# A log-sum-exp over 128 MB on one core: VectorE weighs and sums 4 MB blocks in one go, with a wider filler matmul, a bf16 pass in the closing check, and batch 6's logarithm at the end

## The chip, the core and the metric

The kernel runs on one core of one Trainium2 chip. The core has five engines that run their own instruction streams and meet at semaphores: TensorE (PE: matmuls, PEld: its weight loads), VectorE (DVE), ScalarE (ACT), GpSimd (POOL) and SyncE (SP, which here only issues DMAs). SBUF is the memory on the core with 128 partitions, PSUM the one that TensorE writes. The metric is the time of one execution on the device, in microseconds (us).

## The reference

```python
B, S, D, H = 8, 2048, 2048, 8          # x: 8 x 2048 x 2048 f32, bias: 8 x 256 f32
x_heads = x.reshape(B, S, H, Dh).transpose(0, 2, 1, 3) + bias[None, :, None, :]
x_tiled = np.repeat(x_heads, 2, axis=2)
mx = x_tiled.max(axis=-1, keepdims=True)
lse = mx.squeeze(-1) + np.log(np.exp(x_tiled - mx).sum(axis=-1))
```

Each row of x has 8 heads of 256 numbers. Each head gets its own bias, and the result is the logarithm of the sum of the exponentials, written twice in a row. 128 MB (134 million bytes) are read and 1 MB is written.

## The kernel before

**Tiles.** A tile is 256 rows of x: 128 partitions with K = 2 rows each, 2 MB. There are T = 64 tiles, 8 to a batch. Two neighbouring tiles make a block of 4 MB; four block buffers (xb) hold eight tiles. Tiles 2 to 41 are loaded as whole blocks (L174), the others one by one or in pieces (L185, L193). SP issues a load only when the buffer's last users are done (last_uses, in load and reload).

**The sum without a maximum.** The kernel takes exp without subtracting the maximum, sums, and takes the logarithm. At the end it looks at the largest and smallest sum (ends_of, L532 and L535; judge) and branches to a slow version (all_again) when they lie too far apart. That branch isn't taken here.

**How a bulk tile (0 to 53, BULK) is split by heads.** The loop over t writes the order out by hand; each engine runs its instructions in that order.

- Heads 0 to 2 go through PE: a matmul with ones and the bias in three bf16 parts puts the bias into PSUM (put_bias, L310), and matmuls with the identity add x (late_heads, L369; f32, so each is two passes). ScalarE exponentiates from PSUM: head 0 with its sum (L380, twice), heads 1 and 2 back into xb (L387).
- Heads 4 to 7 get their bias from POOL (g_add, L419).
- ScalarE exponentiates heads 3 to 7 in place (L425, in later).
- VectorE multiplies head 3 by exp(bias) (L437) and sums heads 1 to 7 (L444). This sum is the last use of the buffer, and SP waits for it.

In step t of the loop the order is: PE's matmuls of t, POOL's add of t, the exponential (L425), multiply and sum of tile **t - 1** (flush of for_pool), the exponentials from PSUM of t (L380, L387), and the bias for t + 1.

**The logarithm of a batch.** Two steps after a batch's last tile, finish turns its sums R with four PE transposes (L504), and ScalarE takes the logarithm of the result (L514). It stands at the end of step t = 8b + 9, so in ScalarE's order it comes ahead of the exponential L425 of tile 8b + 9. ends_of follows on VectorE. After batch 6 (t = 57) one DMA stores the results of batches 0 to 6 (store, L518); batch 7 has its own transpose, logarithm and store (finish_last, L613 to L620).

**The prompt tiles (54 to 63).** They are handled row by row (one of the two rows in each partition, 1 MB, at a time; tile 63 in smaller pieces): heads 0 and 1 by PE and ScalarE (L327, L345, L400), the rest exponentiated in place and weighed and summed head by head on VectorE (weigh, L460), one head or two folded on POOL (L476, L484) and summed on VectorE (L490). In tiles 55 to 63 keep_warm puts three 128-column matmuls a row (L360), whose result nobody reads, into PE's order. From there on the exponentials are not held back by a step.

**The end.** ends_of(7) on VectorE, then judge: a small vector (L548), two matmuls into one row (L547 and L556), a maximum (L557), and every engine loads the verdict and branches.

```python
        fb, at = divmod(t - 2, NBLK)
        if fb >= 0 and at == NBLK - 1:
            finish(fb)
            ends_of(fb)
            if fb == B - 2:
                store()
```

Of the kernel before, what the change touches and what calls it, by code (L numbers as in the profile page):

```python
# [9 lines left out]
F32 = mybir.dt.float32  # L10
BF16 = mybir.dt.bfloat16
I32 = mybir.dt.int32
ACT = mybir.ActivationFunctionType
# [4 lines left out]
K = 2  # L18
KB = 4
BLOCKS = 42  # L20

NBUF = 8
# [2 lines left out]

NEARLY = 5

NWARM = 3

# [16 lines left out]
SPAN_BITS = 60 << 23  # L46
# [16 lines left out]
def kernel(  # L63
# [30 lines left out]
    w_sb = sb.tile([P, D - W1], F32, name="w_sb")  # L94
    ident = sb.tile([P, P], F32, name="ident")
    ones = sb.tile([1, P], F32, name="ones")
    ones3 = sb.tile([3, P], BF16, name="ones3")
    b3 = sb.tile([3, CPE], BF16, name="b3")
    bparts = sb.tile([1, 3, CPE], BF16, name="bparts")
    brest = sb.tile([1, 2, CPE], F32, name="brest")  # L100

    b_far = sb.tile([1, 1], F32, name="b_far")
    one_bits = sb.tile([1, 1], F32, name="one_bits")
    ends = sb.tile([P, 2], F32, name="ends")
    far = sb.tile([P, 1], F32, name="far")
    verdict = sb.tile([1, 1], I32, name="verdict")

    NR = KB * H * NB

    Rx = [sb.tile([P, 1 + NR + 1], F32, name=f"R{b}") for b in range(B)]  # L110
    R = [r[:, 1 : 1 + NR].rearrange("p (k h n) -> p k h n", k=KB, h=H) for r in Rx[:-1]]
    R_last = Rx[-1][:, 1 : 1 + NR].rearrange("p (h n k) -> p h n k", h=H, n=NBLK)
    res = sb.tile([H * NB, B - 1, P, KB, 2], F32, name="res")
    res_last = sb.tile([P, P, 2], F32, name="res_last")
    xbs = [sb.tile([P, KB, D], F32, name=f"xb{i}") for i in range(NBUF // TB)]
    xts = [xb[:, k : k + K] for xb in xbs for k in range(0, KB, K)]
# [18 lines left out]
    def rows_of(t, n=1):  # L135


        b, at = divmod(t, NBLK)
        if b < B - 1:
            blk, i = divmod(at, TB)  # L140
            v = x[b, blk * P * KB : (blk + 1) * P * KB, :]
            return v.rearrange("(p k) d -> p k d", k=KB)[:, i * K : (i + n) * K]
        v = x[b, at * P * K : (at + 1) * P * K, :]
        return v.rearrange("(k p) d -> p k d", k=K)


# [53 lines left out]
    def reload(t):  # L200

        n = t + NBUF
        if n < BLOCKS:
            if n % TB == TB - 1:
                load(n - TB + 1)
        elif n < T:
            load(n)

# [4 lines left out]
    for set_idx, (_name, funcs) in enumerate(get_activation_tables(nc.m.arch).items()):  # L213
        if ACT.Exp in funcs and ACT.Ln in funcs:
# [5 lines left out]
            )  # L220
            break
    nc.scalar.dma_start(out=brow, in_=bias.rearrange("h j -> (h j)").unsqueeze(0))
    for t in range(NBUF):
        load(t)
    nc.vector.memset(ones, 1.0)
    nc.vector.memset(ones3, 1.0)
    make_identity(nc, ident)


    bp = brow[:, 0:CPE]  # L230
# [15 lines left out]
    for i, c in enumerate(range(G0, D, MM)):  # L246
# [9 lines left out]
    nc.vector.memset(one_bits, float(ONE_BITS))  # L256
    nc.vector.tensor_reduce(
        out=b_far,
        in_=brow,
        op=ALU.max,  # L260
        axis=mybir.AxisListType.X,
        apply_absolute_value=True,
    )
    nc.vector.tensor_scalar(
        out=Rx[0][0:1, 1 + NR :],
        in0=b_far,
        scalar1=BIAS_MAX,
        scalar2=TOO_FAR,
# [27 lines left out]
    def put_bias(m, k0, k1):  # L296

        if m["late"]:  # L300
            pair = pairs[n_ps[0] % 2]
            n_ps[0] += 1
            got = [one_ps, pair[:, 0:MM], pair[:, MM : 2 * MM]]

            parts = [(ones3, b3)]
            if n_ps[0] <= NEARLY:
                parts = [(ones3[0:1], bparts[:, i]) for i in range(3)]
            for h, p in enumerate(got):
                for i, (lhsT, b) in enumerate(parts):
                    nc.tensor.matmul(  # L310
                        p,
                        lhsT=lhsT,
                        rhs=each_row(b, h * Dh, Dh, K),
                        start=i == 0,
                        stop=False,
                    )
            return got + [pair]
        n = m["pe"] * Dh
        rows = min(k1 - k0, max(MM // n, 1))
        got = []  # L320
        for k in range(k0, k1, rows):
            for c in range(0, n, MM):
                w = min(n - c, MM)
                bank = n_ps[0] % len(ps)
                p = ps[bank][:, 0 : rows * w]
                n_ps[0] += 1
                mm = nc.tensor.matmul(  # L327
                    p,
                    lhsT=ones3,
                    rhs=each_row(b3, c, w, rows),  # L330
                    start=True,
                    stop=False,
                )
                on_bank(bank, mm)
                got.append((k, k + rows, c, w, bank, p))
        return got
# [19 lines left out]
        return heads  # L356

    def keep_warm():
        for _ in range(NWARM):
            nc.tensor.matmul(  # L360
                tp[:, 0], lhsT=ident, rhs=ident, start=True, stop=True
            )

    def late_heads(m, t, got, sums):

# [58 lines left out]
    def exp_inplace(t, v, after):  # L424
        return on_x(t, nc.scalar.activation(out=v, in_=v, func=ACT.Exp), [after])  # L425

    def later(m, t, k0, k1, sums, add):

        h0 = m["pe"] if m["late"] else m["g0"]
        v = xts[t % NBUF][:, k0:k1, h0 * Dh : D]  # L430
        done = exp_inplace(t, v, add)
        if m["late"]:
            n = (m["g0"] - h0) * Dh
            f = v[:, :, 0:n]
            h0 = m["acc"]
            v = xts[t % NBUF][:, k0:k1, h0 * Dh : D]
            mul = nc.vector.tensor_tensor(  # L437
                out=f,
                in0=f,
                in1=each_row(w_ps, m["pe"] * Dh - W0, n, k1 - k0),  # L440
                op=ALU.mult,
            )
            done = on_x(t, mul, [done])
        red = nc.vector.tensor_reduce(  # L444
            out=sums[:, k0:k1, h0:H],
            in_=v.rearrange("p k (h j) -> p k h j", j=Dh),
            op=ALU.add,
            axis=mybir.AxisListType.X,
        )
        last_uses[t].append(on_x(t, red, [done]))  # L450

    def weigh(t, v, h, dst, after):
        c = h * Dh
# [62 lines left out]
    def store():  # L516

        nc.sync.dma_start(  # L518
            out=out[0 : B - 1].rearrange("b h (n r) -> (h n) b r", n=NB),
            in_=res.rearrange("q b p k r -> q b (p k r)"),  # L520
        )

# [17 lines left out]
            negate=b == B - 1,  # L540
        )

    def judge():


        row = w_ps[0:1, 0:P]
        nc.tensor.matmul(row, lhsT=one_bits, rhs=ones, start=True, stop=False)  # L547
        nc.vector.scalar_tensor_tensor(  # L548
            out=far,
            in0=ends[:, 1:2],  # L550
            scalar=-2.0 * ONE_BITS,
            in1=ends[:, 0:1],
            op0=ALU.add,
            op1=ALU.max,
        )
        nc.tensor.matmul(row, lhsT=far, rhs=ident, start=False, stop=True)  # L556
        nc.vector.tensor_reduce(  # L557
            out=verdict, in_=row, op=ALU.max, axis=mybir.AxisListType.X
        )
        return nc.values_load(  # L560
            verdict,
            min_val=0,
            max_val=(1 << 31) - 1,
            skip_runtime_bounds_check_because="it is only compared, and addresses nothing",
        )

    def all_again():
# [12 lines left out]
        with tc.For_i(0, B, 1) as b, tc.For_i(0, S // P, 1) as n:  # L580
# [27 lines left out]
                out=outs[at].rearrange("b n p h r -> (b n p) h r"), in_=both  # L608
            )

    def finish_last():
# [12 lines left out]


    def sums_of(t):

        b, blk = divmod(t, NBLK)
        if b < B - 1:
            return R[b][:, blk % TB * K :, :, blk // TB]  # L630
        return R_last[:, :, blk, :].rearrange("p h k -> p k h")


# [13 lines left out]
    def flush(later_work):  # L647
        for f in later_work:
            f()
        later_work.clear()  # L650

    for t in range(T):
# [66 lines left out]
                for_pe.append(lambda t=t: reload(t))  # L719

        fb, at = divmod(t - 2, NBLK)
        if fb >= 0 and at == NBLK - 1:
            finish(fb)
            ends_of(fb)
            if fb == B - 2:
                store()
    flush(for_pe)
    flush(for_pool)
    finish_last()
    ends_of(B - 1)  # L730
    again = judge() > SPAN_BITS

    order.__exit__(None, None, None)
    with tc.If(again, preferred_fallthrough_block=False):
# [31 lines left out]
```

## Time and profile before

| what | value |
|---|---|
| time, median of 3 runs | 327.25 us (326.83 to 327.27) |
| the profiled execution: its time / its span on the core | 326.85 us / 325.1 us |
| busy: PE, DVE, ACT, POOL | 86%, 89%, 82%, 87% of the span |
| time of the x queue's packets, as a share of 16 DMA engines | 98.1% |
| read from HBM / mean rate | 134.23 MB / 416 GB/s |
| TensorE clock granted, mean | 0.918 |
| chain of waits that ended last: DMA / PE / DVE / ACT | 41% / 21% / 20% / 14% |
| SP waiting for VectorE's sums ahead of 4 MB loads | 174.2 us in 17 waits |
| last piece of x landed / last sum on VectorE done / end of span | 319.1 / 320.4 / 325.1 us |

The span runs from the first instruction of the program to the last. A row of a timeline holds the start in us, the duration in us, the engine, the line of the kernel, the operation, and what it writes and reads; in brackets stands how long the engine had been idle and who ended that. A row of groups ends with the total busy time, the mean of one in ns, and the idle time ahead of them. In a table by stage each engine has its busy time and, in brackets, its instructions; then come the granted clock, the DMA engines' busy share and their rate. Busy shares over the whole span mix stages with different limits, so they are read stage by stage.

### The profile page before, as it was taken

The numbers are of one execution on the slowest core, as the hardware profiler recorded it, in microseconds if no ns is written. First come the engines' busy times: TensorE is split into PE (matmuls) and PEld (weight loads), VectorE is DVE, ScalarE is ACT, GpSimd is POOL, SyncE is SP. The second block draws the span as 40 slices with busy tenths as digits, with TensorE's granted clock in tenths as the row PEclk, the third lists the DMA queues.
The fourth block names the chain that finished last, engine by engine and source line by source line (L and its number), as shares of the span: only waits on it lengthen the run. The fifth ranks groups of instructions, "written<-read, shape, count | busy, mean of one in ns | idle before, by whom it ended". The sixth has DMA issues, their size and how long they took to land.

```text
span 325.1 us, 2588 instructions
## 1 busy us (share of the span) xinstructions
PE 278.4 (86%) x728; PEld 107.1 (33%) x728; DVE 288.2 (89%) x356; ACT 266.9 (82%) x438; POOL 284.3 (87%) x141
## 2 busy tenths in 40 slices
PE   5999999889977869888669799698988888899984
PEld 2333333323322323323223333233333332355452
DVE  1355679999999998999997999999999999999985
ACT  1167679889978977879886989868998899989994
POOL 7939997999999999999999999999999995886872
PEclk9977789989997998979996989987999799799998
DMA  7999999999999999999999999999999999999993
GB/s 306 466 395 448 448 401 441 444 423 423 448 427 415 447 427 415 448 435 404 448 444 398 448 444 419 417 423 425 431 425 428 421 430 419 422 413 419 420 397 113
DMA packets 8849, 135.46 MB, mean 417 GB/s; under 512 B 1057, under 2 KB 1441, under 8 KB 2433
## 3 DMA queue, kind: packets, MB, share of 16 engines
q1 hardware_dynamic: 8736, 135.27, 98.1%
q8 instruction: 6, 0.10, 0.1%
q14 instruction: 9, 0.07, 0.1%
q10 hardware_dynamic: 98, 0.01, 0.0%
HBM read 134.23 MB, written 1.05 MB: 416 GB/s over the span
## 4 chain that ended last, share of the span: by engine, by line
DMA 41%; PE 21%; DVE 20%; ACT 14%; POOL 1%; issue 1%; SPq 0%
DMA xb<-in_x_dram 41%; DVE R L444 17%; PE pair L369 9%; ACT xb L425 8%; PE one_ps L369 5%; PE pair L310 3%; DVE xb L437 3%; ACT xb L387 2%; PE one_ps L310 2%; ACT xb L380 2%; POOL xb L419 1%; PE pair L242 1%; ACT res L514 1%; PE tp L504 1%; DMA brow<-in_bias_dram 1%
## 5 line engine op out<-in xcount | busy, mean ns | idle before, releaser
L419 POOL TENSOR_TENSOR xb<-xb,b_rep 128x2048 f32<-128x2048 f32 x54 | 243.7, 4536 | 20.3 <-DMA xb<-in_x_dram 20.3
L444 DVE TENSOR_REDUCE R<-xb 128x14 f32<-128x3584 f32 x54 | 209.9, 3888 | 1.9
L425 ACT ACTIVATE xb<-xb 128x2560 f32<-128x2560 f32 (+5 forms) x77 | 156.8, 2039 | 8.9 <-POOL xb L419 8.3
L369 PE MATMUL pair<-xb,ident 128*128 128x512 f32 x216 | 118.6, 678 | 0.0
L387 ACT ACTIVATE xb<-pair 128x1024 f32<-128x1024 f32 x54 | 55.9, 1034 | 24.7 <-PE pair L369 24.6
L369 PE MATMUL one_ps<-xb,ident 128*128 128x512 f32 x108 | 67.4, 709 | 9.3 <-DMA xb<-in_x_dram 9.2
L369 PEld LDWEIGHTS pair<-xb,ident 128*128 128x128 f32 x216 | 47.5, 220 | 63.0 <-issue 63.0
L437 DVE TENSOR_TENSOR xb<-xb,w_ps 128x512 f32<-128x512 f32 x54 | 36.7, 680 | 23.2 <-ACT xb L425 23.2
L380 ACT ACTIVATE xb<-one_ps 128x256 f32<-128x256 f32 x108 | 40.3, 386 | 5.9 <-PE one_ps L369 5.9
L310 PEld LDWEIGHTS <-ones 3*128 3x128 bf16 (+1 forms) x192 | 16.7, 95 | 80.3 <-issue 70.9
L310 PE MATMUL one_ps<-b,ones 3*128 3x512 bf16 x49 | 18.9, 386 | 23.4 <-ACT xb L380 23.3
L310 PE MATMUL pair<-b,ones 3*128 3x512 bf16 x98 | 28.9, 374 | 0.0
L460 DVE CUSTOM_DVE_ANT_0 xb<-xb,w_ps 128x256 f32<-128x256 f32 x79 | 28.5, 416 | 0.1
L369 PEld LDWEIGHTS one_ps<-xb,ident 128*128 128x128 f32 x108 | 16.9, 197 | 31.7 <-DMA xb<-in_x_dram 15.9
L345 PE MATMUL pair<-xb,ident 128*128 128x512 f32 (+1 forms) x42 | 21.9, 604 | 4.5 <-DMA xb<-in_x_dram 4.5
L484 POOL TENSOR_TENSOR xb<-xb 128x128 f32<-128x128 f32 (+3 forms) x57 | 20.1, 352 | 4.5
L380 ACT ACTIVATION_READ_ACCUMULATOR xb<-one_ps 128x1 f32 x108 | 22.9, 212 | 0.0
L476 POOL TENSOR_TENSOR xb<-xb,w_sb 128x256 f32<-128x256 f32 (+1 forms) x19 | 14.4, 759 | 8.2 <-ACT xb L425 7.4
L360 PE MATMUL tp<-ident 128*128 128x128 f32 x108 | 17.4, 300 | 0.0
L360 PEld LDWEIGHTS tp<-ident 128*128 128x128 f32 x108 | 14.1, 198 | 4.4 <-issue 3.9
L400 ACT ACTIVATE xb<-pair 128x256 f32<-128x256 f32 x39 | 14.4, 379 | 0.0
L514 ACT ACTIVATE res<-tp 32x1024 f32<-32x1024 f32 x7 | 7.1, 1013 | 6.4 <-PE tp L504 6.4
(55 smaller groups left out, 94.8 us busy)
## 6 DMA issues: line engine op xcount, KB each, us to landing
xb<-in_x_dram SPq DMA_DIRECT2D x20, 4096.0 KB, 21.8
xb<-in_x_dram SPq DMA_DIRECT2D x16, 2048.0 KB, 21.9
xb<-in_x_dram SPq DMA_DIRECT2D x14, 1024.0 KB, 20.7
xb<-in_x_dram SPq DMA_DIRECT2D x4, 256.0 KB, 12.4
out_dram<-res SPq DMA_DIRECT2D x1, 896.0 KB, 7.7
xb<-in_x_dram SPq DMA_DIRECT2D x2, 384.0 KB, 16.8
xb<-in_x_dram SPq DMA_DIRECT2D x2, 128.0 KB, 7.4
out_dram<-res_last SPq DMA_DIRECT2D x1, 128.0 KB, 1.7
```

The costliest lines, as they stand in the source:

```text
L310: nc.tensor.matmul(p, lhsT=lhsT, rhs=each_row(b, h * Dh, Dh, K), start=i == 0, stop=False,)
L345: mm = nc.tensor.matmul(p, lhsT=ident, rhs=xts[t % NBUF][:, ka:kb, c : c + w], start=False, stop=True,)
L360: nc.tensor.matmul(tp[:, 0], lhsT=ident, rhs=ident, start=True, stop=True)
L369: mm = nc.tensor.matmul(p, lhsT=ident, rhs=xts[t % NBUF][:, :, h * Dh : (h + 1) * Dh], start=False, stop=True,)
L380: act = nc.scalar.activation(out=xts[t % NBUF][:, k, 0:Dh], in_=got[0][:, k * Dh : (k + 1) * Dh], func=ACT.Exp, accum_out=sums[:, k, 0:1],)
L387: act = nc.scalar.activation(out=xts[t % NBUF][:, :, Dh : m["pe"] * Dh].rearrange("p k (h j) -> p h k j", j=Dh), in_=got[-1].rearrange("p ...
L419: add = nc.gpsimd.tensor_tensor(out=v, in0=v, in1=each_row(b_rep, c - G0, D - c, k1 - k0), op=ALU.add)
L425: return on_x(t, nc.scalar.activation(out=v, in_=v, func=ACT.Exp), [after])
L437: mul = nc.vector.tensor_tensor(out=f, in0=f, in1=each_row(w_ps, m["pe"] * Dh - W0, n, k1 - k0), op=ALU.mult,)
L444: red = nc.vector.tensor_reduce(out=sums[:, k0:k1, h0:H], in_=v.rearrange("p k (h j) -> p k h j", j=Dh), op=ALU.add, axis=mybir.AxisListTy ...
L460: ttr = nc.vector.tensor_tensor_reduce(out=v, in0=v, in1=w, scale=1.0, scalar=0.0, op0=ALU.mult, op1=ALU.add, accum_out=dst,)
L484: done = nc.gpsimd.tensor_tensor(out=v[:, :, 0:n], in0=v[:, :, 0:n], in1=v[:, :, n : 2 * n], op=ALU.add)
```

## The change

- Tiles 2 to 41 (those loaded as 4 MB blocks): VectorE's multiply and sum are issued once a block, at its second tile, over both tiles; the even tile issues only its exponential. The block's buffer is free after that one sum. Tiles 42 to 49, which go into such buffers, are loaded two by two.
- The three filler matmuls of 128 columns become one of 384 columns with the bias rows as data.
- The bias matmul (L310, L327) runs over 128 rows, 125 of them zero, instead of 3; five first tiles keep their one-row form.
- The largest bias is found on 8 partitions from a second copy of the bias (b8) instead of on one.
- The verdict's two matmuls run in bf16; the first is issued ahead of the last tile's sums.
- Batch 6 gets its own layout: tiles are 256 rows in a row, its sums are turned by two transposes and its logarithm and store (128 KB) come after the last tile's work. The store of the other batches (0 to 5) and the ends of batch 6 move from step 57 to step 61.

```diff
-NWARM = 3
+WARM = 384
...
-    ones3 = sb.tile([3, P], BF16, name="ones3")
-    b3 = sb.tile([3, CPE], BF16, name="b3")
+    ones_bf = sb.tile([P, P], BF16, name="ones_bf")
+    b3 = sb.tile([P, CPE], BF16, name="b3")
...
+        elif n < BLOCKS + NBUF:
+            if n % TB == TB - 1:
+                for i in range(n - TB + 1, n + 1):
+                    load(i)
         elif n < T:
             load(n)
...
+    nc.scalar.dma_start(out=b8, in_=bias)
...
+    nc.vector.memset(ones_bf, 1.0)
+    nc.vector.memset(b3, 0.0)
     make_identity(nc, ident)
+    nc.gpsimd.tensor_copy(ident_bf, ident)
...
     nc.vector.tensor_reduce(
         out=b_far,
-        in_=brow,
+        in_=b8,
...
-            parts = [(ones3, b3)]
+            parts = [(ones_bf, b3)]
...
     def keep_warm():
-        for _ in range(NWARM):
-            nc.tensor.matmul(
-                tp[:, 0], lhsT=ident, rhs=ident, start=True, stop=True
-            )
+        nc.tensor.matmul(
+            tp[:, 0 : WARM // P], lhsT=ident, rhs=b_rep[:, 0:WARM], start=True, stop=True
+        )
...
         done = exp_inplace(t, v, add)
+        tiles = [t]
+        if TB <= t < BLOCKS:
+            if t % TB < TB - 1:
+                return
+            tiles = range(t - TB + 1, t + 1)
+            xt, k0, k1 = xbs[t // TB % len(xbs)], 0, KB
+            sums = R[t // NBLK][:, :, :, t % NBLK // TB]
+        else:
+            xt = xts[t % NBUF]
         if m["late"]:
             n = (m["g0"] - h0) * Dh
-            f = v[:, :, 0:n]
+            f = xt[:, k0:k1, h0 * Dh : m["g0"] * Dh]
             h0 = m["acc"]
-            v = xts[t % NBUF][:, k0:k1, h0 * Dh : D]
+            v = xt[:, k0:k1, h0 * Dh : D]
...
-        last_uses[t].append(on_x(t, red, [done]))
+        on_x(t, red, [done])
+        for u in tiles:
+            last_uses[u].append(red)
...
-            out=out[0 : B - 1].rearrange("b h (n r) -> (h n) b r", n=NB),
+            out=out[0 : B - 2].rearrange("b h (n r) -> (h n) b r", n=NB),
...
-    def judge():
-        row = w_ps[0:1, 0:P]
-        nc.tensor.matmul(row, lhsT=one_bits, rhs=ones, start=True, stop=False)
+    def begin_row():
+        row = one_ps[0:1, 0:P]
+        nc.tensor.matmul(row, lhsT=one_bits, rhs=ones_bf[0:1], start=True, stop=False)
+        return row
...
-        nc.tensor.matmul(row, lhsT=far, rhs=ident, start=False, stop=True)
+        nc.tensor.matmul(row, lhsT=far, rhs=ident_bf, start=False, stop=True)
...
+    def turn_two():
+        for k in range(K):
+            nc.tensor.transpose(
+                out=tp[0 : H * NBLK, 1 + k],
+                in_=R[B - 2][:, k].rearrange("p h n -> p (h n)"),
+                identity=ident,
+            )
+
+    def finish_two():
...
+        nc.scalar.activation(out=res_two, in_=tv, func=ACT.Ln)
+        nc.sync.dma_start(
+            out=out[B - 2].rearrange("h (n r) -> (h n) r", n=NBLK),
+            in_=res_two.rearrange("q p k r -> q (p k r)"),
+        )
...
-        if fb >= 0 and at == NBLK - 1:
+        if 0 <= fb < B - 2 and at == NBLK - 1:
             finish(fb)
             ends_of(fb)
-            if fb == B - 2:
-                store()
+        if t == T - 3:
+            ends_of(B - 2)
+            store()
+    row = begin_row()
     flush(for_pe)
     flush(for_pool)
+    turn_two()
+    finish_two()
     finish_last()
     ends_of(B - 1)
-    again = judge() > SPAN_BITS
+    again = judge(row) > SPAN_BITS
```

More of the change, by code (lines that the diff above doesn't have):

```diff
@@ L96 @@
     ones = sb.tile([1, P], F32, name="ones")
-    ones3 = sb.tile([3, P], BF16, name="ones3")
-    b3 = sb.tile([3, CPE], BF16, name="b3")
+    ones_bf = sb.tile([P, P], BF16, name="ones_bf")
+    b3 = sb.tile([P, CPE], BF16, name="b3")
     bparts = sb.tile([1, 3, CPE], BF16, name="bparts")
     brest = sb.tile([1, 2, CPE], F32, name="brest")
-    b_far = sb.tile([1, 1], F32, name="b_far")
-    one_bits = sb.tile([1, 1], F32, name="one_bits")
+    b8 = sb.tile([H, Dh], F32, name="b8")
+    b_far = sb.tile([H, 1], F32, name="b_far")
+    ident_bf = sb.tile([P, P], BF16, name="ident_bf")
+    one_bits = sb.tile([1, 1], BF16, name="one_bits")
     ends = sb.tile([P, 2], F32, name="ends")
-    far = sb.tile([P, 1], F32, name="far")
+    far = sb.tile([P, 1], BF16, name="far")
     verdict = sb.tile([1, 1], I32, name="verdict")
@@ L110 @@
     Rx = [sb.tile([P, 1 + NR + 1], F32, name=f"R{b}") for b in range(B)]
-    R = [r[:, 1 : 1 + NR].rearrange("p (k h n) -> p k h n", k=KB, h=H) for r in Rx[:-1]]
+    R = [r[:, 1 : 1 + NR].rearrange("p (k h n) -> p k h n", k=KB, h=H) for r in Rx[:-2]]
+    R.append(Rx[-2][:, 1 : 1 + NR].rearrange("p (k h n) -> p k h n", k=K, h=H))
     R_last = Rx[-1][:, 1 : 1 + NR].rearrange("p (h n k) -> p h n k", h=H, n=NBLK)
-    res = sb.tile([H * NB, B - 1, P, KB, 2], F32, name="res")
+    res = sb.tile([H * NB, B - 2, P, KB, 2], F32, name="res")
+    res_two = sb.tile([H * NBLK, P, K, 2], F32, name="res_two")
     res_last = sb.tile([P, P, 2], F32, name="res_last")
@@ L138, in rows_of @@
         b, at = divmod(t, NBLK)
-        if b < B - 1:
+        if b < B - 2:
             blk, i = divmod(at, TB)
@@ L143, in rows_of @@
         v = x[b, at * P * K : (at + 1) * P * K, :]
+        if b == B - 2:
+            return v.rearrange("(p k) d -> p k d", k=K)
         return v.rearrange("(k p) d -> p k d", k=K)
@@ L225 @@
     nc.vector.memset(ones, 1.0)
-    nc.vector.memset(ones3, 1.0)
+    nc.vector.memset(ones_bf, 1.0)
+    nc.vector.memset(b3, 0.0)
     make_identity(nc, ident)
+    nc.gpsimd.tensor_copy(ident_bf, ident)
     bp = brow[:, 0:CPE]
@@ L264 @@
     nc.vector.tensor_scalar(
-        out=Rx[0][0:1, 1 + NR :],
+        out=Rx[0][0:H, 1 + NR :],
         in0=b_far,
@@ L303, in put_bias @@
             got = [one_ps, pair[:, 0:MM], pair[:, MM : 2 * MM]]
-            parts = [(ones3, b3)]
+            parts = [(ones_bf, b3)]
             if n_ps[0] <= NEARLY:
-                parts = [(ones3[0:1], bparts[:, i]) for i in range(3)]
+                parts = [(ones_bf[0:1], bparts[:, i]) for i in range(3)]
             for h, p in enumerate(got):
@@ L328, in put_bias @@
                     p,
-                    lhsT=ones3,
+                    lhsT=ones_bf,
                     rhs=each_row(b3, c, w, rows),
@@ L541, in ends_of, with judge @@
         )
-    def judge():
-        row = w_ps[0:1, 0:P]
-        nc.tensor.matmul(row, lhsT=one_bits, rhs=ones, start=True, stop=False)
+    def begin_row():
+        row = one_ps[0:1, 0:P]
+        nc.tensor.matmul(row, lhsT=one_bits, rhs=ones_bf[0:1], start=True, stop=False)
+        return row
+    def judge(row):
         nc.vector.scalar_tensor_tensor(
@@ L609, in all_again @@
             )
+    def turn_two():
[6 more added lines that the diff above has]
+    def finish_two():
+        two = tp[0 : H * NBLK, 1]
+        tv = bass.AP(
+            tensor=two.tensor, offset=two.offset, ap=[two.ap[0], [1, P], [P, K], [0, 2]]
+        )
[3 more added lines that the diff above has]
+            in_=res_two.rearrange("q p k r -> q (p k r)"),
+        )
     def finish_last():
@@ L628, in sums_of @@
         b, blk = divmod(t, NBLK)
-        if b < B - 1:
+        if b < B - 2:
             return R[b][:, blk % TB * K :, :, blk // TB]
+        if b == B - 2:
+            return R[b][:, :, :, blk]
         return R_last[:, :, blk, :].rearrange("p h k -> p k h")
```

## The prediction

> **What bounds the kernel now.** I read the page first, then the wait list of SP's queue, then VectorE's timeline, then the neighbourhood of the first logarithm. The page:
>
> ```profile
> PE 278.4 (86%) x728; PEld 107.1 (33%) x728; DVE 288.2 (89%) x356; ACT 266.9 (82%) x438; POOL 284.3 (87%) x141
> ...
> q1 hardware_dynamic: 8736, 135.27, 98.1%
> ...
> L419 POOL TENSOR_TENSOR xb<-xb,b_rep 128x2048 f32<-128x2048 f32 x54 | 243.7, 4536 | 20.3 <-DMA xb<-in_x_dram 20.3
> L444 DVE TENSOR_REDUCE R<-xb 128x14 f32<-128x3584 f32 x54 | 209.9, 3888 | 1.9
> ```
>
> The transfers are busy all the time (98.1%), so the x loads set the end; but VectorE (DVE) is close behind. POOL's adds that wait for a landing start at 102.07, 111.80, 121.53: a 4 MB block lands every 9.73 us. VectorE needs 4.51 us a tile, 9.03 us a block (starts 240.47 and 244.99 below). It is ahead by only 0.7 us a block, and at the end of the bulk it has no idle time at all:
>
> ```profile
> 240.47 0.68 DVE L437 TENSOR_TENSOR xb<-xb,w_ps 128x512 f32<-128x512 f32 x1
> 241.19 3.89 DVE L444 TENSOR_REDUCE R<-xb 128x14 f32<-128x3584 f32 x1
> 244.99 0.68 DVE L437 TENSOR_TENSOR xb<-xb,w_ps 128x512 f32<-128x512 f32 x1
> ```
>
> After the bulk (last reduce 277.69 + 3.89 = 281.58), the table by stage leaves VectorE this much room up to its last reduce at 320.42:
>
> ```profile
> 281.60:290.00 8.40, 8.40 (x51) 0.99 1.01 421
> 290.00:300.00 10.00, 10.00 (x63) 1.00 1.01 415
> 300.00:310.00 10.00, 9.61 (x58) 1.00 1.02 423
> 310.00:318.00 8.00, 7.12 (x42) 1.00 1.03 383
> 318.00:320.50 2.50, 2.29 (x15) 1.00 0.46 161
> ```
>
> The second figure is busy time: 37.4 of 38.8 us. VectorE has **1.4 us** of slack from 281.58 on. Whatever makes it later than that at 281.58 makes the end later.
>
> **Part 1: the pair on VectorE.** Removed: for tiles 2 to 41, 20 multiplies and 20 reduces. What a pair costs: a reduce of 2048 elements takes 2.27 us (L257), one of 3584 takes 3.89, so 1.054 ns an element and 0.11 fixed; 7168 give 7.65 us. The multiply, 512 elements in 0.68, holds 0.14 fixed; 1024 give 1.22. With the 0.03 between them a pair takes 8.9 us, and the next starts 0.1 before its end: 8.8 in a row, against 9.03. Neither size is in the trace; bounds are 8.7 (both fixed parts saved and more) and 9.1 (nothing saved). Gain 0.2 a pair, 4 us of VectorE's work in all.
>
> **Part 2: the wait it adds.** The multiply of an even tile now waits for the exponential of the odd one. Queued behind it on VectorE is only the next work; waiting for its reduce are SP's load of that buffer and, once a batch, PE's transposes (L504), ScalarE's logarithm (L514), and all that ScalarE has after it. The first logarithm today:
>
> ```profile
> 60.14 3.89 DVE L444 TENSOR_REDUCE R<-xb 128x14 f32<-128x3584 f32 x1
> 63.94 0.68 DVE L437 TENSOR_TENSOR xb<-xb,w_ps 128x512 f32<-128x512 f32 x1
> 64.65 3.89 DVE L444 TENSOR_REDUCE R<-xb 128x14 f32<-128x3584 f32 x1
> ```
> ```profile
> 64.08 0.40 PE L504 MATMUL tp<-ident,R 128*32 128x128 f32 x2 [0.86 <-DVE R L444]
> ```
> ```profile
> 64.51 1.01 ACT L514 ACTIVATE res<-tp 32x1024 f32<-32x1024 f32 x1 [1.55 <-PE tp L504]
> 65.43 2.32 ACT L425 ACTIVATE xb<-xb 128x2560 f32<-128x2560 f32 x1
> ```
>
> Tile 7's reduce ends at 64.03; PE transposes at 64.08, the logarithm starts at 64.51, and only then comes tile 9's exponential (65.43 to 67.75). VectorE loses nothing now, because tile 8 lies ready and covers it (63.94). After the change tile 8 can't be touched before tile 9's exponential: the cover is gone. From the end X of the pair's reduce: 0.04, four transposes and their way to ScalarE 0.67 (two take 0.43, each more 0.12), logarithm to exponential 0.92, exponential 2.32, 0.03: the next pair starts at X + 4.0 and ends at X + 12.9. The ends of the batch (L532, L535) lie in the gap. A batch of four pairs takes 12.9 + 3 x 8.8 = **39.3 us**; the transfers bring one in 4 x 9.73 = 38.9. So VectorE becomes the bound, and the lateness it starts with stays.
>
> **Part 3: the sum along VectorE.** Tiles 0 and 1 are single, as now. Tile 3's exponential lets VectorE start at 39.59 (its multiply today); until then it idles where tile 2 was done.
>
> - (2,3): 39.6 to 48.5. (4,5): tile 5's exponential ends 47.35 + 2.36 = 49.71; ends 58.6. (6,7): ends 67.4, now 64.0.
> - Four batches more, 39.3 each: (38,39) ends 224.6. Then X + 12.9: (40,41) ends 237.5, now 222.83 + 3.89 = 226.7.
> - Tiles 42 to 53 stay single, and VectorE now does them almost without idle (0.2) in 54.9 us: ends 292.2 against 281.58, 10.6 late.
> - The last stages absorb 1.4. The closing reduce L532 today starts 0.2 after VectorE is free (it waits for ScalarE); gone too. Left: 10.6 - 1.6 = +9.0.
>
> **The other edits.** The verdict: L556 is two f32 passes, the second 0.11 after the first; one bf16 pass saves 0.1, on the path. Batch 6's logarithm moves off ScalarE's row (1.01 us and 1.37 idle at 292.4) to the end: 512 elements lie between 256 (0.38) and 1024 (1.01), so 0.6 after the last sums; hidden, as ScalarE will be some us ahead of VectorE. If it weren't: two store issues of 0.36 in SP's queue, and the last store, which lands 1.7 after its issue at 321.42, comes 0.2 to 0.4 later. The first store shrinks by an eighth, -0.2 at most on the last loads, and those no longer decide. The 384-column matmul streams the same columns; PE waits there for data: 0. Bias matmuls over 128 rows for 3: the same 512 columns; bounds 0 and twice 0.37 each, +0.65 of PE a tile beside a cadence of 3.9 (58.23 to 62.10 of L310) under 4.9: hidden. The added start-up work (8 KB more bias, two memsets, one copy) lies before brow lands at 2.6 or in VectorE's idle time; the shorter L257 too: 0. Batch 6's rows come in the same 16 KB runs: 0.
>
> The loads: the shortest time from issue to landing is 17.8 us now. With the releases above the worst is the load of tiles 40 and 41: today it is issued at 189.00 and lands at 208.96 (chain of waits); it would be issued when (32,33) is done, 185.3 + 12.9 = 198.2, and a block needs 9.7 and at least the 1.7 of a small store. So the queue may just run dry, some tenths of a us a batch. VectorE is then some 5 us behind the landings, which covers it.
>
> Sum: +9.0 - 0.1 = +8.9 on the profiled execution (span 325.1, 326.85 with what lies around it): **335.7**. The median of the runs is 0.4 above that execution, far below the doubt here.
>
> **A rule weighed.** PE will idle longer at each logarithm. Half clock shows now after far less:
>
> ```profile
> 66.00:70.20 4.20, 2.73 (x8) 1.00 0.98 421
> 70.20:73.60 3.40, 3.40 (x5) 0.50 1.05 453
> ```
>
> The Trainium skill, "TensorE: Matmul & The Clock Gate", section "HAM oscillation", says that an idle gap of over about 3.4 us throttles PE. Here a stretch with PE 65% busy sufficed, so trace and rule differ. By the rule only the changed kernel would pay it, by the row both do.
>
> **Rivals.**
>
> A, the sum above; with pairs of 8.7 or 9.1 (20 pairs, 0.1 is 2 us) 333.8 to 341.4. Chance 0.50.
>
> B, the start's lateness is made up, since a pair costs 8.5 or less and a batch under 38: then (38,39) follows its landing (199.30, two adds 9.03, exponential 2.33, 8.9) and ends at 219.6, 5 us sooner: 330.7. Against: the fixed parts are small. 0.17.
>
> C, **not slower**: the late release is all there is, and the loads' lead of 17.8 to 22 us hides it; VectorE's saved 4 us pay for the gaps. It decides as soon as VectorE is at most 1.4 us late at 281.58. For: VectorE idles 23 us on ScalarE's exponentials today. Against: most of that lies before 50 us, and ScalarE runs in order. Only the verdict and the store are left: 326.85 - 0.1 - 0.2 = 326.5. 0.18.
>
> D, PE at half clock after each longer stall: six passes at 0.85 for 0.43 us put tile 8b+11's exponential 2.5 later, past VectorE's need by 1.8, four times: up to 342.9. 0.10. Something else 0.05.
>
> The range takes A, B and C: 326.3 to 340.0. A alone: 333.8 to 340. A measurement tells about 0.2% (0.65 us) from no change: C is split 0.11 within and 0.07 faster; with the rest, faster 0.07, same 0.13, slower 0.80.
>
> **What would show it.** Right: in VectorE's timeline a gap of about 4 us before the multiply of every fourth pair, L504 waiting 4 us on DVE, VectorE without idle after 292, last x landing 8 us before the last reduce, transfers idle at the end. Wrong: pairs at 8.5 or less, exponentials of tiles 9, 17, 25 not after the logarithm, or last reduces following the landing by 1.4 us as today.

## The result, and the profile after

| | before | after |
|---|---|---|
| time, median | 327.26 us (326.83 to 327.48, 4 runs) | 335.22 us (334.54 to 335.68, 4 runs) |
| the profiled execution: time / span | 326.85 / 325.1 us | 335.51 / 333.7 us |
| busy, of the span: PE, DVE, ACT, POOL | 86%, 89%, 82%, 87% | 78%, 84%, 79%, 85% |
| last piece of x landed / last sum on VectorE done | 319.06 / 320.42 us | 323.19 / 329.52 us |
| TensorE clock granted, mean | 0.918 | 0.924 |

The changed kernel takes 1.024 times as long (95% interval 1.0221 to 1.0265): some 8 us more. Every engine is busy for a smaller share, so something waits. These lines of the page after answer to those of before: section 3 (packets, MB, share), section 4 (the chain that ended last), and the group of VectorE's sums.

```profile
q1 hardware_dynamic: 8784, 135.27, 96.6%
...
DVE 75%; PE 14%; ACT 8%; DMA 1%; issue 0%; DVEq 0%
...
L467 DVE TENSOR_REDUCE R<-xb 128x28 f32<-128x7168 f32 (+1 forms) x34 | 206.9, 6084 | 1.2
```

The chain that ended last went 41% through DMA and 20% through VectorE; now it is 1% and 75%. The transfers are no longer busy all the time. The bound has moved to VectorE, though VectorE does less (281.6 us busy instead of 288.2). The page's groups hide why, since the reduce's own line shows 1.2 us of idle time ahead of it; the table of waits (in all, times, longest) tells more:

```profile
DVE xb L460 <- ACT xb L437: 40.6, 8, 11.6
ACT res L539 <- PE tp L529: 30.8, 6, 8.0
...
PE tp L529 <- DVE R L467: 25.1, 7, 4.5
```

Read upwards, this is a ring. PE's transposes wait for VectorE's sum, ScalarE's logarithm for the transposes, and VectorE's next multiply for an exponential that ScalarE has queued behind the logarithm. One turn of it in VectorE's timeline, at the first logarithm, where before tile 8's multiply followed at 63.94 without a gap:

```profile
59.11 7.62 DVE L467 TENSOR_REDUCE R<-xb 128x28 f32<-128x7168 f32 x1
66.76 0.29 DVE L557 TENSOR_REDUCE R<-R 128x1 int32<-128x129 int32 x1
66.97 0.28 DVE L560 TENSOR_REDUCE R<-R 128x1 int32<-128x129 int32 x1
71.13 1.22 DVE L460 TENSOR_TENSOR xb<-xb,w_ps 128x1024 f32<-128x1024 f32 x1 [3.89 <-ACT xb L437]
72.39 7.62 DVE L467 TENSOR_REDUCE R<-xb 128x28 f32<-128x7168 f32 x1
79.92 1.21 DVE L460 TENSOR_TENSOR xb<-xb,w_ps 128x1024 f32<-128x1024 f32 x1
```

And the other two sides, in the timelines of PE and of ScalarE:

```profile
66.78 1.04 PE L529 MATMUL tp<-ident,R 128*32 128x128 f32 x4 [4.55 <-DVE R L467]
```
```profile
67.86 1.01 ACT L539 ACTIVATE res<-tp 32x1024 f32<-32x1024 f32 x1 [5.57 <-PE tp L529]
68.78 2.32 ACT L437 ACTIVATE xb<-xb 128x2560 f32<-128x2560 f32 x1
```

The sum ends at 66.73, the logarithm runs from 67.86, the exponential that the next pair needs (L437) from 68.78 to 71.10, and the multiply at 71.13. Four more gaps follow before 110.75, 150.57, 189.77 and 229.40 (3.88, 3.88, 3.46, 3.89). At the end the table by stage (busy time and instructions of PE, PEld, DVE, ACT, POOL; then clock, DMA share, rate) shows VectorE without idle time and the transfers thinning out:

```profile
300.00:310.00 10.00, 8.94 (x25) 4.25 (x25) 10.00 (x63) 10.00 (x25) 8.31 (x21) 1.00 1.01 417
310.00:318.00 8.00, 6.57 (x21) 2.86 (x18) 8.00 (x52) 8.00 (x20) 6.76 (x15) 1.00 1.01 406
318.00:326.00 8.00, 5.51 (x14) 2.53 (x15) 8.00 (x49) 8.00 (x22) 6.53 (x14) 0.88 0.70 221
```

### The profile page after: what moved, and what is told of

Same layout as the page of the kernel before. It is cut to its first block, busy times and chain, and to the rows that moved or that the text cites. A ratio compares the mean times of both kernels' runs of the same rounds, so it can differ in the third digit from the quotient of the medians.

```text
span 333.7 us, 2399 instructions
## 1 busy us (share of the span) xinstructions
PE 259.2 (78%) x652; PEld 106.9 (32%) x652; DVE 281.6 (84%) x317; ACT 264.4 (79%) x438; POOL 284.7 (85%) x142
## 4 chain that ended last, share of the span: by engine, by line
DVE 75%; PE 14%; ACT 8%; DMA 1%; issue 0%; DVEq 0%
DVE R L467 55%; DVE xb L485 10%; DVE xb L460 8%; ACT xb L437 5%; PE pair L381 5%; PE one_ps L381 2%; PE pair L323 2%; PE tp L529 1%; PE one_ps L323 1%; PE pair L255 1%; ACT res L539 1%; ACT xb L399 1%; DMA brow<-in_bias_dram 1%; DVE R L515 1%; ACT xb L392 0%
## 5 line engine op out<-in xcount | busy, mean ns | idle before, releaser
L467 DVE TENSOR_REDUCE R<-xb 128x28 f32<-128x7168 f32 (+1 forms) x34 | 206.9, 6084 | 1.2
L437 ACT ACTIVATE xb<-xb 128x2560 f32<-128x2560 f32 (+5 forms) x77 | 159.5, 2088 | 3.4 <-POOL xb L431 3.3
L381 PE MATMUL pair<-xb,ident 128*128 128x512 f32 x216 | 112.6, 648 | 0.0
L460 DVE TENSOR_TENSOR xb<-xb,w_ps 128x1024 f32<-128x1024 f32 (+1 forms) x34 | 33.8, 994 | 40.7 <-ACT xb L437 40.6
L381 PE MATMUL one_ps<-xb,ident 128*128 128x512 f32 x108 | 62.8, 666 | 6.4 <-DMA xb<-in_x_dram 6.4
L323 PEld LDWEIGHTS <-ones_bf 128*128 128x128 bf16 (+1 forms) x192 | 18.7, 99 | 78.6 <-issue 69.5
L323 PE MATMUL one_ps<-b,ones_bf 128*128 128x512 bf16 x49 | 18.5, 377 | 26.5 <-ACT xb L392 26.4
L323 PE MATMUL pair<-b,ones_bf 128*128 128x512 bf16 x98 | 29.1, 378 | 0.0
L381 PEld LDWEIGHTS one_ps<-xb,ident 128*128 128x128 f32 x108 | 20.8, 207 | 17.2 <-DMA xb<-in_x_dram 8.8
L529 PE MATMUL tp<-ident,R 128*32 128x128 f32 x24 | 5.8, 379 | 25.1 <-DVE R L467 25.1
L372 PE MATMUL tp<-b_rep,ident 128*128 128x384 f32 x36 | 15.3, 508 | 0.0
```

Source lines behind the costliest of these rows:

```text
L323: nc.tensor.matmul(p, lhsT=lhsT, rhs=each_row(b, h * Dh, Dh, K), start=i == 0, stop=False,)
L381: mm = nc.tensor.matmul(p, lhsT=ident, rhs=xts[t % NBUF][:, :, h * Dh : (h + 1) * Dh], start=False, stop=True,)
L460: mul = nc.vector.tensor_tensor(out=f, in0=f, in1=each_row(w_ps, m["pe"] * Dh - W0, n, k1 - k0), op=ALU.mult,)
L467: red = nc.vector.tensor_reduce(out=sums[:, k0:k1, h0:H], in_=v.rearrange("p k (h j) -> p k h j", j=Dh), op=ALU.add, axis=mybir.AxisListTy ...
```

## The experiments

The theory is the prediction's: **the stall**, once a batch, because the pair takes away the finished tile that used to cover the logarithm, and, beside it, VectorE's late start. The rivals: **the loads** (the later release of a block runs the queue dry), **the others** (the clock, the closing check, batch 6's layout), and the pair's own length.

### The changed kernel, VectorE by tile again

```diff
-        if TB <= t < BLOCKS:
+        if False:
...
-        elif n < BLOCKS + NBUF:
-            if n % TB == TB - 1:
-                for i in range(n - TB + 1, n + 1):
-                    load(i)
```

> The changed kernel with VectorE's multiply and sum by tile again; every other edit stays. Three theories. Stall: VectorE's sum of a block ends later, the batch's logarithm waits for it and holds back ScalarE, and VectorE then idles some 3.9 us a batch. Loads: the block's buffer comes free later, the transfers run dry, and the late data set the end. Others: one of the other edits costs the 8 us. Stall and loads both expect 326.3 to 327.5 us here (before: 327.3; small gains of 0.1 for the verdict, up to 0.2 for the smaller store). Others expects 333 to 335.5.

Measured: 327.02 us (326.82 to 327.14), 1.0000 of before (0.9991 to 1.0010). The whole loss goes with the pair. The other edits together are worth nothing that can be measured; "the others" is out. One thing they do change: TensorE's granted clock is 0.948 to 0.967 in these ten runs, against 0.916 to 0.940 in those of the kernel before. Which of them does that was not taken apart, and it buys no time here.

### The kernel before, with the pair alone

```diff
+        if TB <= t < BLOCKS:
+            if t % TB < TB - 1:
+                return
+            tiles = range(t - TB + 1, t + 1)
+            xt, k0, k1 = xbs[t // TB % len(xbs)], 0, KB
+            sums = R[t // NBLK][:, :, :, t % NBLK // TB]
```

> The kernel before with the pair on VectorE alone (multiply and sum once a block, and tiles 42 to 49 loaded two by two). Stall and loads: 334.5 to 336.5 us, VectorE idle 3.9 us after each batch's ends, as in the changed kernel. Others: 327 to 328.

Measured: 336.34 us, 1.0295 (1.0278 to 1.0312). The same five gaps stand before L452, 3.88 us each. The median is 1.1 us above that of the full change. The two profiled executions are 0.6 apart (spans of 334.3 and 333.7), and there the traces tell why: 0.37 is the wait for the verdict's matmul (0.68 us idle ahead of it here, 0.31 in the changed kernel, 0.47 in the kernel before), and 0.2 is the fourth gap, 3.88 here and 3.46 in the changed kernel (VectorE was 0.1 to 0.2 earlier here up to that gap, and its last pair starts at 229.63 instead of 229.40). The other 0.5 lies between executions that were not profiled.

### The changed kernel, the logarithm one step later

```diff
-        fb, at = divmod(t - 2, NBLK)
+        fb, at = divmod(t - 3, NBLK)
```

> The changed kernel with the transposes, logarithm and ends of a batch one step later (after step 8b + 10), so that the exponential of tile 8b + 9 is issued ahead of the logarithm; the pairs stay, and so do the late releases. Stall: the gap of 3.9 us on VectorE goes, VectorE catches up with the landings, then tile 41's sum follows its landing: 208.96 + 0.07 + two adds 9.06 + exponential 2.33 + pair 8.9 = 229.3 against 226.7 before; 1.6 of the 2.6 are absorbed at the end: 327.5 to 328.5 us. Loads: the release of a block still comes a whole pair late, the transfers still run dry at the start: 331 to 335.

Measured: 327.01 us (326.78 to 327.29), 1.0004 (0.9994 to 1.0013). The pairs are all there, and so is the late release; only the place of the logarithm in ScalarE's order is another. VectorE's timeline at the batch's end:

```profile
68.67 7.62 DVE L467 TENSOR_REDUCE R<-xb 128x28 f32<-128x7168 f32 x1
76.21 0.28 DVE L557 TENSOR_REDUCE R<-R 128x1 int32<-128x129 int32 x1
76.41 0.28 DVE L560 TENSOR_REDUCE R<-R 128x1 int32<-128x129 int32 x1
76.60 1.21 DVE L460 TENSOR_TENSOR xb<-xb,w_ps 128x1024 f32<-128x1024 f32 x1
```

The next multiply follows at once. So the pair as such, and the later release of a block (67.51 for tiles 6 and 7, where tile 7 was done at 64.03), cost nothing that can be measured; the stall is the loss. It was 0.5 us better than the least I had expected. But VectorE has nothing to spare in it: from 281.6 to 318.0 it shows no idle time, where the kernel before had 1.4 us. The equal time is close to a tie between loads and VectorE, not slack: the last piece of x lands at 318.39, and VectorE's last sum ends 2.4 us later, where the kernel before needs 1.4.

### The kernel before, the logarithm one step earlier

```diff
-        fb, at = divmod(t - 2, NBLK)
+        fb, at = divmod(t - 1, NBLK)
```

> The kernel before, VectorE by tile, with the transposes, logarithm and ends one step earlier (after step 8b + 8): the logarithm then waits for a sum of VectorE's that has only just been issued, and stands ahead of the exponential of tile 8b + 8. No pair and no later release except what the stall makes. Stall: VectorE idles 3.8 us a batch; a batch takes 8 x 4.515 + 3.8 = 39.9 against 38.9 for its data; tile 47's sum 9.4 later than before, one more gap: 12.8 late at the end of the bulk, 1.6 absorbed: 338 us, and up to 343 as batch 6's logarithm then waits as well. Loads and others: 327 to 328.

Measured: 343.44 us (340.29 to 343.63), 1.051 (1.0493 to 1.0528). There is no pair in this kernel, and the gap is there all the same:

```profile
56.54 3.89 DVE L444 TENSOR_REDUCE R<-xb 128x14 f32<-128x3584 f32 x1
60.46 0.29 DVE L532 TENSOR_REDUCE R<-R 128x1 int32<-128x129 int32 x1
60.66 0.28 DVE L535 TENSOR_REDUCE R<-R 128x1 int32<-128x129 int32 x1
64.39 0.69 DVE L437 TENSOR_TENSOR xb<-xb,w_ps 128x512 f32<-128x512 f32 x1 [3.46 <-ACT xb L425]
```

3.46 us idle, six times. The median lies 0.4 us above the 343 that I had put as the most. The profiled execution, at 340.29 us, is the fastest of the five; the others took 343.43 to 343.63 at a slightly lower granted clock (0.883 to 0.896 instead of 0.900), and what they lose beyond it is in no trace. The stall comes from the distance between a batch's last sum and its logarithm, counted in pieces of VectorE's work that lie ready; the pair is one way of taking that distance away.

### Pairs for half of the blocks

```diff
-        if TB <= t < BLOCKS:
+        if TB <= t < 26:
```
```diff
-        if TB <= t < BLOCKS:
+        if 26 <= t < BLOCKS:
```

The first of them also loses the loading two by two of tiles 42 to 49.

> The changed kernel with pairs for tiles 2 to 25 alone; from tile 26 VectorE works by tile, and loads go one by one after it. Two stalls that count are left (after tiles 7 and 15; at the third logarithm tile 24 is in a pair still, so perhaps a third). Stall alone: VectorE is some 8 to 12 us late at tile 25 and makes up 0.4 us a tile and more against the data from there: hardly late at the end of the bulk, 327 to 328 us. Stall with dry transfers: what the transfers lost by then (2.6 us in the changed kernel, at the loads behind the first two stalls) is never made up, since they are the bound again: last piece of x lands at 321.5 to 322.5 instead of 319.1, and 329 to 330.5 us.

> The changed kernel with pairs for tiles 26 to 41 alone; the start is by tile as before. Tests the part of the sum that the start lays in. Stall: pairs follow their landings until the logarithm after tile 31; then two stalls: (38,39) ends 219.8, (40,41) 232.7 against 226.7 before; 6.0 late, 1.6 to 1.8 absorbed: 331 to 331.5 us, between before (327) and the changed kernel (335.2). The transfers don't run dry. If stalls simply added up without regard to the data, two of them would cost 2 x 3.9 - 1.6 = 6.2: 333. If the early tiles made all the loss: 327.

Measured: pairs up to tile 25, 330.69 us, 1.0112 (1.0095 to 1.0129), three gaps of 3.88; pairs from tile 26 on, 331.42 us, 1.0145 (1.0128 to 1.0162), gaps of 3.88 and 3.46 after two logarithms (and before them 4.29 once, where the first pair waits for its second tile). Two late stalls cost about as much as three early ones.

In the second kernel the transfers never ran dry (the last piece of x lands at 318.02), and the loss is VectorE's lateness itself. In the first, the numbers are about those that I had put for a stall with dry transfers: the last piece lands at 321.97, 2.9 us after that of the kernel before, and the time is 0.2 above the 330.5 expected at most. But its trace doesn't show the transfers as the cause. The chain that ended last holds next to no transfer:

```profile
DVE 75%; PE 15%; ACT 7%; DMA 1%; issue 1%; DVEq 0%
```

VectorE's last sum ends at 325.94, 4.0 us after the last landing (1.4 in the kernel before). Between 193.58 and that sum VectorE waits for nothing, and the wait that ends at 193.58 is not for a landing either:

```profile
191.29 0.28 DVE L553 TENSOR_REDUCE R<-R 128x1 int32<-128x129 int32 x1
191.49 0.28 DVE L556 TENSOR_REDUCE R<-R 128x1 int32<-128x129 int32 x1
193.58 0.69 DVE L456 TENSOR_TENSOR xb<-xb,w_ps 128x512 f32<-128x512 f32 x1 [1.81 <-ACT xb L433]
```
```profile
178.46 0.81 ACT L287 ACTIVATE w_ps<-b_rep 128x768 f32<-128x768 f32 x1 [5.98 <-DVE xb L456]
```

Tile 33, which starts here, had landed at 173.26. ScalarE stood for 5.98 us at the factors that it writes once, in step 32 (L287), until VectorE's late multiply had read the old ones; tile 33's exponential came after that and after the next logarithm. VectorE is 9.3 us later at this tile than in the kernel before (193.58 instead of 184.32), 7.7 at the end of the bulk (289.26 instead of 281.58) and 5.5 at the last sum. So an early lateness is not made up either, since in the kernel before VectorE itself waits for exponentials for no more than 1.0 us from 200 us on. "The loads" is not the cause here: what the transfers lost stays hidden behind VectorE. This is the slowest of the four executions (331.77 us); the faster ones were not profiled.

### The price of a dry queue

Two kernels with nothing but the 32 loads of 4 MB, into one buffer or into two; the output is filled with zeros.

```python
xbs = [sb.tile([P, KB, D], F32, name=f"xb{i}") for i in range(1)]   # or range(2)
for i in range(B * NB):
    b, at = divmod(i, NB)
    v = x[b, at * P * KB : (at + 1) * P * KB, :]
    nc.sync.dma_start(out=xbs[i % 1], in_=v.rearrange("(p k) d -> p k d", k=KB))   # or i % 2
```

> Not the reference's work: 32 blocks of 4 MB are loaded into one buffer, each load after the landing of the one before; nothing is computed and the output is zeros. A block is then 9.73 us of data plus all that a load costs when nothing is queued. As in the prediction (1.7 us of a small store): 11.4 us a block, 366 us. As the changed kernel's dry places suggest (issued 80.07, 2.7 before the landing before it, landed 1.4 later than in step): 13.8 us a block, 443 us.

> Not the reference's work: the same with two buffers, so that a load is issued when the one ahead of it has just begun. Any price of 1.7 or 4.1 us a load is then hidden: 9.73 us a block, 313 to 316 us.

Measured: 397.62 us with one buffer, 319.48 us with two (one run each). The pages' last sections, with the KB of a load and the median from issue to landing:

```profile
xb<-in_x_dram SPq DMA_DIRECT2D x32, 4096.0 KB, 12.2
```
```profile
xb<-in_x_dram SPq DMA_DIRECT2D x32, 4096.0 KB, 19.4
```

With two buffers a block lands every 9.70 to 9.73 us, so 19.4 is two of them; the time is 3.5 us above the most that I had expected, because the first block lands only at 15.65. Alone, a load takes 12.2: **2.5 us** above 9.72. That is neither of the two values that I had set against each other. In the changed kernel the price is not one number. Take a load's lead, the time from its issue to the landing of the load ahead of it, and its loss, what its landing comes later than 9.72 after that one: the load issued at 80.07 had a lead of 2.71 and lost 1.41; that of 159.51 had 3.73 and lost 0.95. Over all the kernels that compute, as far as the traces tell both landings, leads of 1.9 to 3.7 always lost (0.34 to 1.79), leads of 4.1 to 5.6 lost between nothing and 1.44, and leads of 5.97 to 6.52 nothing. Longer leads lost nothing to 0.14, with three exceptions: 0.53 at a lead of 8.78 (the pair alone), 0.53 at 12.96 (the changed kernel by tile), 1.13 at 24.56 (the logarithm one step earlier). So a part of the scatter has nothing to do with the lead. Why two equal leads (4.53 and 4.52 in the kernel with pairs up to tile 25) lost 0 and 1.17 stays open.

### Both answers at once

The runs point to a logarithm one step later, and to whole loads for four more tiles. Both with the pairs and, in the second, without.

```diff
-WHOLE = (54, 55)
+WHOLE = (54, 55, 56, 57, 58, 59)
...
-        fb, at = divmod(t - 2, NBLK)
+        fb, at = divmod(t - 3, NBLK)
```

> The changed kernel with both answers that the runs point to: the logarithm one step later (t - 3, as in e3), and tiles 56 to 59 loaded whole (2 MB) instead of row by row, since in the trace a 2 MB load adds 4.905 us to the landings and two of 1 MB 2 x 2.494. If the loads alone set the end, as the stall theory has it once the stall is gone, the last landing comes 4 x 0.08 = 0.3 us sooner and the time is 326.7, at most 0.1% below before. If VectorE is still what bounds, the later landing of each tile's first row (2.5 us) hurts its row-by-row work in tiles 56 to 59 and the time is 327 or above.

> The same without the pairs (VectorE by tile, logarithm at t - 3, tiles 56 to 59 whole). The pairs' saved work (some 4 us of VectorE's busy time) is worth nothing where the loads set the end, so 326.7 as with the pairs; if saved work on VectorE matters, this one is later than the one with pairs, by up to 1 us.

Measured: 327.09 us with pairs, 1.0009 (0.9994 to 1.0024); 326.97 us by tile, 0.9999 (0.9990 to 1.0007). Neither beats the kernel before. Of the two cases for the first, it is the one in which VectorE still bounds; for the second neither came, since it is as fast as the first and at 327.0. In the first (whose profiled execution took 327.84 us, 0.75 above its median) the table by stage shows VectorE busy throughout:

```profile
290.00:300.00 10.00, 7.44 (x21) 3.28 (x20) 10.00 (x63) 8.65 (x22) 7.04 (x17) 1.00 1.01 420
300.00:310.00 10.00, 8.87 (x25) 3.67 (x23) 10.00 (x62) 10.00 (x24) 8.29 (x21) 1.00 1.01 416
```

and in the second VectorE has room:

```profile
290.00:300.00 10.00, 7.44 (x21) 3.27 (x20) 9.17 (x58) 8.65 (x21) 7.05 (x17) 1.00 1.01 419
300.00:310.00 10.00, 8.79 (x25) 3.66 (x23) 8.86 (x54) 10.00 (x24) 8.27 (x21) 1.00 1.01 417
```

DVE is the third engine: 10.00 of 10.00 and 10.00 of 10.00, against 9.17 and 8.86. The same holds without the whole loads: VectorE ends the bulk at 284.15 with pairs and the later logarithm, and at 281.34 in the changed kernel by tile. Although a pair is less work than two tiles, a kernel with pairs comes out of the bulk with VectorE later. The 0.3 us that the whole loads should save shows in neither time, though the last piece does land sooner (317.42 and 318.32, against 319.06 before).

## Why the prediction was right

The forecast was 335.7, the measured median 335.22, and A, the sum along VectorE, is the case that came. The range, 326.3 to 340.0, also held "not slower", so the time alone says little; what tells A from C are the gaps.

- **The pair.** Forecast 8.9, and 8.8 in a row; measured 1.21 to 1.22 + 7.62, and 8.78 to 8.79 in a row (79.92 to 88.70). The two sizes that the trace of before didn't show followed from a slope and a fixed part taken from its rows. B needed 8.5 and is out.
- **The stall.** Forecast: the next pair at X + 4.0 and its end at X + 12.9, the pieces in between read off one logarithm of the kernel before. Measured X + 4.40 from the end of the reduce (66.73 to 71.13), and X + 13.28 to its end. The forecast was 0.4 short: four transposes and their way to ScalarE took 1.1 (66.78 to 67.86), not 0.67, at half clock, as the last point shows. The batch: forecast 39.3, measured 39.6, 39.8, 39.6 and 39.2. The kernel with the later logarithm shows that without this stall the loss is nothing.
- **The sum.** Forecast against measured: (6,7) 67.4 and 66.7; (38,39) 224.6 and 225.0; (40,41) 237.5 and 238.3; tile 53 292.2 and 292.84, that is 11.3 late instead of 10.6. Of this the stages at the end absorbed 2.2 (36.7 us from there to the last sum, instead of 38.8), where the forecast had 1.4: work that was busy for 37.4 us between its waits takes 36.7 without any. Two terms were off by 0.7 and 0.8, with opposite signs, so the last sum is 9.1 late; that they cancel is luck. From there to the end 0.5 us is saved, of which 0.1 is the gap ahead of the closing reduce and 0.16 the verdict's wait: +8.6 on the span, where I had +8.9.
- **The verdict.** Forecast -0.1, measured -0.16 (0.47 to 0.31 idle).
- **C's point** was VectorE at most 1.4 us late at the end of the bulk. It was 11 late. In the kernel with the later logarithm it was 2.6 late (284.15 instead of 281.58), more than C allowed, and yet about C's time came, 327.01: there too the last stages absorbed 2.2, since VectorE's last sum ends only 0.4 later than in the kernel before (320.83 instead of 320.42). So the 1.4 us of slack was the mis-sized term.
- **The loads** were mis-sized. I had priced a dry queue at 1.7 at least and "some tenths of a us a batch". The transfers lost 4.1 us in all (323.19 against 319.06), the single places up to 1.41, and a load alone costs 2.5. For the same reason the last landing was 6.3 us before the last sum, not 8. The place was wrong too: the load of tiles 40 and 41, named as the worst, was issued at 198.71 (forecast 198.2) and delayed nothing that landed after it; the worst is the load of 80.07. None of this changed the forecast's time, because VectorE waited for something else at every one of these places.
- **D and the rule weighed.** In the changed kernel PE does drop to half clock, at four of the five stalls. The stage table around the first and the fourth, with the clock in the column after POOL:

```profile
61.20:64.61 3.41, 0.81 (x3) 0.19 (x2) 3.41 (x1) 1.09 (x3) 2.26 (x2) 1.00 1.03 442
64.61:68.02 3.41, 1.24 (x5) 0.98 (x6) 2.60 (x3) 0.16 (x1) 3.41 (x2) 0.50 1.07 461
68.02:71.44 3.42, 3.42 (x5) 1.35 (x4) 0.31 (x1) 3.42 (x5) 3.42 (x1) 0.50 1.04 450
180.66:184.08 3.42, 1.79 (x6) 0.44 (x4) 3.42 (x1) 2.69 (x6) 2.56 (x2) 1.00 1.02 441
184.08:187.49 3.41, 1.64 (x7) 0.99 (x8) 2.20 (x3) 0.99 (x2) 3.41 (x1) 1.00 0.96 413
```

The fourth stall, the short one of 3.46 ahead of 189.77, is the counterexample. Its four transposes took 0.61 us, those of the first (above) 1.04:

```profile
185.85 0.61 PE L529 MATMUL tp<-ident,R 128*32 128x128 f32 x4 [2.56 <-DVE R L467]
```

The logarithm then starts 0.65 after the transposes (185.85 to 186.50) instead of 1.08, and the pair at X + 4.0 (185.79 to 189.77), which is the forecast's number. So the missing 0.4 a batch is the clock. I had given the rule no term in the sum; it was worth four times 0.4 us.

The length of PE's single wait does not decide on it, though. At the five stalls of the changed kernel PE had been idle for 4.55, 3.93, 3.59, 2.56 and 3.50 us, and only the fourth kept the full clock. By itself this would agree with the limit of about 3.4 us in the Trainium skill, "TensorE: Matmul & The Clock Gate", section "HAM oscillation"; the other runs don't. With the pair alone, PE's transposes ran at half clock after waits of 4.56, 2.49, 3.18, 2.67 and 1.30 us; with pairs from tile 26 on they ran at half clock after 1.89 and at full clock after 2.93. What the traces do show is a grid: within each of them the granted clock changes only at multiples of 3.41 us from one another. In the changed kernel, from 40 us on, it left full speed after each step of this grid in which PE was busy for 1.45 us or less, and kept it after all with 1.64 or more, the two around the fourth stall among them. In the kernel before and in the one with the pair alone, half clock also followed steps with up to 2.3 us of busy PE; why they differ was not tested.

D's further step, a second gap at the exponential two tiles on, came once and small. After the second stall ScalarE waited 1.15 us for matmuls that PE did at half clock, and the pair that follows the first one starts at 119.73, 0.1 after the sum ahead of it (112.01 + 7.62) instead of 0.1 before that sum's end: this is the batch of 39.8.

What the experiments leave open: the 0.5 us by which the other executions of the pair alone are slower, the 3 us by which those of the earlier logarithm are, the size of a dry queue's loss at equal leads, and what beside PE's busy time sets its clock.

## What to carry to other kernels

Before two instructions become one, look for what used to run between them: a small chain through other engines (here sum, transposes, logarithm, then the exponential in the same in-order queue) is free only while a finished piece of work covers it, and fewer, larger pieces remove the cover before they save anything. Find it by following the ring once through the trace of before, with the ready work taken out, and move the small chain one step later if it can wait. Price a late release by the queue's lead as well, but see in the chain that ended last whether the transfers set the end at all: in every slower kernel of this case, whether its transfers had lost time or not, VectorE has 64% to 78% of that chain and DMA 1% to 14%. An engine makes up a lateness only out of its own idle time.

## What the runs showed of the hardware

- The granted clock of PE changed only on a grid of 3.41 us. Half clock, for one to three steps of it, followed steps in which PE was little busy (1.45 us or less in the changed kernel), and cost 0.4 us in a chain that holds only four short transposes of PE's (1.04 us instead of 0.61). A single wait's length told nothing: half clock came after 1.30 us and full clock after 2.93.
- A 4 MB load by itself took 12.0 to 12.5 us from issue to landing, in a queue that holds another one 9.72: 2.5 us apart. Loads issued up to 3.7 us ahead of the landing before them always lost something, those 5.97 to 6.52 us ahead nothing; but single loads with leads of 8.78, 12.96 and 24.56 lost 0.5 to 1.1 as well.
- VectorE's sum of 7168 f32 elements per partition took 7.62 us and of 3584 took 3.89: 0.16 us fixed, by the difference. The multiply of 1024 took 1.21 and of 512 took 0.68: 0.15 fixed.
